# Two trunk layers on one core: attention given scheduler priority, S5's C products in alternation, softmax sums applied to the results

## The chip, the core and the metric

The kernel runs on one core of one Trainium2 chip (trn2). The time is device microseconds of one launch, from the first to the last instruction and the little that lies around them. Engines are TensorE (PE for its products, PEld for its weight loads), VectorE (DVE), ScalarE (ACT), GpSimd (POOL) and SyncE (SP), which here issues all transfers. TensorE's granted clock has two levels in the rows below, 1.2 and 2.4 GHz; the column PEclk shows them as 0.50 and 1.00, or a mixture over a stretch.

## What is computed

Two layers over 640 tokens of width 1024 (128 of a prompt, 512 of a sample grid of 8 rows by 64 columns). In each layer a normalised and modulated input goes through one projection (w_in); its parts feed three groups of heads; their outputs go through one projection (w_out), a normalisation, a SwiGLU feed-forward block and another normalisation. Cut to what matters here:

```python
def attend_dense(q, k, v):                      # GQA: 8 query heads, 2 key heads, 640 keys
    s = jnp.einsum('bqgrd,bkgd->bgrqk', qi, k) * scale
    p = jax.nn.softmax(s, axis=-1)
    return jnp.einsum('bgrqk,bkgd->bqgrd', p, v)
...
    # na_latent (NA): 4 heads, 256 local keys with a bias table and 128 context keys
    p = jax.nn.softmax(jnp.concatenate([s_loc, s_ctx], axis=-1), axis=-1)
    o = einsum(p_loc, vg) + einsum(p_ctx, cv)
...
    # ssm_mixer (S5): 16 groups of 16 channels, 64 complex states, two directions
    hs = ssm_scan(uf, lam_bar, b_bar, h0, rev)
    y = y + jnp.einsum('blgp,gcp->blgc', hs, c_mat).real
...
    o = jnp.concatenate([ssm_out, na_out, gqa_out], axis=-1) @ lp['w_out']
```

## The kernel before, in words

Tokens lie in 5 tiles of 128. Weights are split into two float32r halves, `wh` and `wl`, and three products (`mm3`, L311 to L313) make one. `Build.layer` runs a layer up to w_out, `Build.ffn` the rest; the second layer's modulation and S5 tables are made beside the first one's feed-forward block.

**The order of the work** is set by a scheduler at build time: each instruction has a priority by its place in the program, and among those that are ready in its own timeline the scheduler takes the one with the best priority. Each engine then runs its list in that order and waits at the head of it. So the program's order is a preference, and the lists that the build gives are the real order.

**The attention stage** of a layer is the part that the change touches. `layer` walks 18 GQA units through `pipelined` (L983 on), depth 1: the front of unit n, then the back of unit n-1, then `between`, which feeds in pieces of S5, of the remaining w_in products (`fill`), of the modulation (`ada`) and of the first layer's S5 tables. After that come 10 NA units, depth 2, with the rest of S5 between them, and then `wout`.

A GQA unit (`gqa_units.front`, L1139 on) takes a tile and two heads. For each head PE makes 128x640 scores (L1149) into one of two two-bank PSUM tiles `psS`; DVE takes the row maximum (L1152) and scales it (L1153); ACT makes the exponential with the row sum beside it (L1156); DVE takes the reciprocal (L1158), and POOL, or for one head of the second layer DVE, multiplies the 128x640 probabilities by it (L1162, L1160). The tables `SCG` and `SCN` choose that engine. The back (L1166 on) transposes the probabilities in ten 128x128 blocks through two PSUM tiles `psT` (helper L852), ACT copies them out (L1175), ten products with V follow (L1180; two heads in alternation on the two column halves of PE, 64 columns each), and ACT copies the 128x128 result (L1185). 32 of the 36 units are of this kind; four are a prompt's, of another form.

An NA unit (`na_units.front`, L926 on) is alike with 384 keys: scores L935, L936 and L940, exponentials L948, reciprocal L949, multiplication on POOL (L954) or DVE (L952), transposes, six products with V (L976, alternating too), and a split of the result from PSUM into a high half (ACT, L283) and a low half (DVE, L284). 16 units in the two layers are of this kind.

S5 (`ssm`, L669 on) walks 8 pairs of groups per layer. For a pair, PE makes the inputs (L714) and turns them (L724), DVE rotates, scans and rotates back (L732, L738, L742, L747, L748, L753), and `back` makes the C products (L767) and one product with the direct table (L769): for each of the two groups of the pair four products from a 64-row half of the state tile, then the direct one with 128 rows. The two groups write to two different banks of one `psS`:

```python
for gg in range(2):
    o, ps_ = yp[:, gg], slice(64 * gg, 64 * gg + 64)
    for n, (d, w) in enumerate(((0, 0), (0, 1), (1, 0), (1, 1))):
        nc.tensor.matmul(o, lhsT=sx[ps_, d, w, :], ...)
    nc.tensor.matmul(o, lhsT=ug[:, gg, :], ...)
```

A float32 product stands in the trace as two records; the counts below are of records.

Of the kernel before, what the change touches and what calls it, by code (L numbers as in the profile page):

```python
# [12 lines left out]
ALU = mybir.AluOpType  # L13
# [144 lines left out]
class Build:  # L158
# [510 lines left out]
    def ssm(self, l, zu, T, out):  # L669
# [90 lines left out]
        def back(pair, sx, rot, rml, tcb, tm, ug, vs, c):  # L760

            yp = self.psS()[0:NJ, :, 0:128]
            for gg in range(2):
                o, ps_ = yp[:, gg], slice(64 * gg, 64 * gg + 64)
                for n, (d, w) in enumerate(((0, 0), (0, 1), (1, 0), (1, 1))):
                    q = w * 2 + d
                    nc.tensor.matmul(o, lhsT=sx[ps_, d, w, :], rhs=tcb[ps_, q * 128:(q + 1) * 128], start=(n == 0),  # L767
                                     stop=False)
                nc.tensor.matmul(o, lhsT=ug[:, gg, :], rhs=tm[:, gg * 128:(gg + 1) * 128], start=False, stop=True)  # L769
# [63 lines left out]
    def softmax_prompt(self, sp, nh, P, scq):  # L833
# [13 lines left out]
        V.tensor_tensor(out=P, in0=P, in1=sm[:, 0:nh].unsqueeze(2).broadcast_to([128, nh, 128]), op=ALU.mult)  # L847

# [50 lines left out]
    def na_units(self, l, N, mh, ml):  # L899
# [26 lines left out]
        def front(cb):  # L926
# [23 lines left out]
            for hh in range(2):  # L950
                if self.SCN[l][hh]:
                    V.tensor_scalar(out=P[:, hh], in0=P[:, hh], scalar1=sm[:, hh:hh + 1], scalar2=None, op0=ALU.mult)  # L952
                else:
                    G.tensor_tensor(out=P[:, hh], in0=P[:, hh], in1=sm[:, hh:hh + 1].broadcast_to([128, 384]),  # L954
                                    op=ALU.mult)
            return P

        def back(cb, P):
# [8 lines left out]
            for j in range(3):  # L967
                for hh in range(2):
# [14 lines left out]
    def pipelined(self, units, depth, between=None):  # L983

        live = {}
        for n in range(len(units) + depth):
            if n < len(units):
                live[n] = units[n][0](units[n][2])
            if n >= depth:
                _, back, a = units[n - depth]  # L990
                back(a, live.pop(n - depth))
                if between:
                    between(n - depth)
# [97 lines left out]
    def gqa_units(self, l, kv, zq, K, ss, mixd):  # L1091
# [47 lines left out]
        def front(a):  # L1139
            i, pr = a  # L1140
            qT = prepare(i)
            Ps = []
            for hh in range(2):
# [7 lines left out]
                nm = self.small(1, tag="gm", bufs=4)  # L1151
                V.tensor_reduce(out=nm, in_=sp[:, :, 0:320], axis=AX.XY, op=ALU.max, negate=True)  # L1152
# [742 lines left out]
```

## Time and profile before

| | us |
|---|---|
| median of 3 runs | 1859.57 |
| lowest and highest | 1850.95, 1860.01 |
| the profiled execution, its own time | 1860.72 |
| its span, first to last instruction | 1858.9 |
| mean granted clock over the span | 0.927 of 2.4 GHz |

The span falls into these stretches, by the first and last instructions of each kind: the first layer's modulation and first w_in pieces up to about 125 us; its GQA units from 125 to 340; its NA units and the end of S5 from 340 to about 401, where products of w_out set in; w_out, feed-forward and the next layer's first pieces up to 1090; the second layer's GQA from 1090 to 1240, its NA and S5 from 1240 to 1312; w_out and feed-forward to the end. In the rows below a group of instructions shows its total busy time and the mean of one; "idle before" is the time that its engine stood idle just ahead of it, with what ended that.

### The profile page before, as it was taken

The numbers are of one execution on the slowest core, as the hardware profiler recorded it, in microseconds if no ns is written. First come the engines' busy times: TensorE is split into PE (matmuls) and PEld (weight loads), VectorE is DVE, ScalarE is ACT, GpSimd is POOL, SyncE is SP. The second block draws the span as 40 slices with busy tenths as digits, with TensorE's granted clock in tenths as the row PEclk, the third lists the DMA queues.
The fourth block names the chain that finished last, engine by engine and source line by source line (L and its number), as shares of the span: only waits on it lengthen the run. The fifth ranks groups of instructions, "written<-read, shape, count | busy, mean of one in ns | idle before, by whom it ended". The sixth has DMA issues, their size and how long they took to land. (4 is left out here: it accounts for less than half of the span.)

```text
span 1858.9 us, 31182 instructions
## 1 busy us (share of the span) xinstructions
PE 1694.2 (91%) x11432; PEld 1474.2 (79%) x11432; DVE 1257.5 (68%) x2468; ACT 820.5 (44%) x1780; POOL 847.6 (46%) x723
## 2 busy tenths in 40 slices
PE   5889798899699999999997989999989999999997
PEld 3878577678498879798886978877768898998996
DVE  5466634744758876687978577665467776777777
ACT  5335444554633334242336556544565242433433
POOL 4755524237642616054456344211594473553553
PEclk9879998769799999999999999985889999999999
DMA  8534765535534554432414343453452222312312
GB/s 302 132 93 113 218 197 156 150 121 168 183 107 142 167 158 151 130 110 91 126 57 156 110 110 99 108 159 80 156 189 84 91 83 77 103 58 79 103 57 80
DMA packets 183113, 234.87 MB, mean 126 GB/s; under 512 B 78960, under 2 KB 112048, under 8 KB 182960
## 3 DMA queue, kind: packets, MB, share of 16 engines
q1 hardware_dynamic: 182960, 232.88, 41.0%
q8 instruction: 90, 1.47, 0.3%
q14 instruction: 63, 0.52, 0.1%
HBM read 203.57 MB, written 29.39 MB: 125 GB/s over the span
## 5 line engine op out<-in xcount | busy, mean ns | idle before, releaser
L284 POOL TENSOR_TENSOR wl<-wr,wh 128x512 fp32r<-128x512 f32 x362 | 507.8, 1423 | 464.9 <-ACT wh L283 313.4
L283 ACT CAST wh<-wr 128x512 fp32r<-128x512 f32 x450 | 275.3, 619 | 394.4 <-PE psM L313 101.7
L311 PE MATMUL psM<-hh,wh 128*128 128x320 f32 x560 | 180.1, 322 | 8.9 <-DVE modc L393 2.6
L312 PE MATMUL psM<-hl,wh 128*128 128x320 f32 x560 | 178.3, 318 | 0.0
L313 PE MATMUL psM<-hh,wl 128*128 128x320 f32 x560 | 178.1, 318 | 0.0
L311 PEld LDWEIGHTS psM<-hh,wh 128*128 128x128 f32 x560 | 109.1, 195 | 12.5 <-DVE modc L393 2.8
L1162 POOL TENSOR_TENSOR ys<-ys,sm 128x640 f32<-128x640 f32 x48 | 61.7, 1289 | 120.4 <-DVE sm L1158 89.4
L311 PE MATMUL psT<-hh,wh 128*128 128x320 f32 x352 | 109.8, 312 | 0.0
L313 PEld LDWEIGHTS psM<-hh,wl 128*128 128x128 f32 x560 | 108.7, 194 | 1.4 <-issue 1.4
L312 PEld LDWEIGHTS psM<-hl,wh 128*128 128x128 f32 x560 | 109.0, 195 | 1.0 <-issue 0.7
L313 PE MATMUL psT<-hh,wl 128*128 128x320 f32 x352 | 109.0, 310 | 0.0
L312 PE MATMUL psT<-hl,wh 128*128 128x320 f32 x352 | 108.9, 309 | 0.0
L230 POOL TENSOR_TENSOR sm<-sm,mhalf 128x1 f32<-128x1 f32 (+2 forms) x46 | 54.7, 1191 | 94.2 <-DVE sm L260 53.6
L1152 DVE TENSOR_REDUCE sm<-psS 128x1 f32<-128x640 f32 x64 | 52.0, 819 | 56.0 <-PE psS L1149 55.6
L1629 DVE TENSOR_TENSOR ys<-ys,psM 128x320 f32<-128x320 f32 x140 | 64.9, 481 | 34.8 <-PE psM L313 32.9
L1629 DVE TENSOR_TENSOR ys<-ys,psT 128x320 f32<-128x320 f32 x140 | 65.0, 481 | 30.4 <-PE psT L313 29.3
L311 PE MATMUL psT<-b,wh 128*128 128x320 f32 x240 | 76.9, 320 | 8.9 <-DVE ys L1629 8.9
L852 PE MATMUL psT<-ident,ys 128*128 128x128 f32 x440 | 79.3, 304 | 6.1 <-ACT sm L1185 2.0
L284 POOL TENSOR_TENSOR wl<-ws,wh 128x512 fp32r<-128x512 f32 x40 | 53.7, 1344 | 63.7 <-ACT wh L283 63.7
L311 PE MATMUL psM<-b,wh 128*128 128x320 f32 x240 | 76.6, 319 | 6.2 <-DVE ys L1629 6.2
L311 PE MATMUL psT<-wh,xs 128*128 128x512 f32 x190 | 75.8, 399 | 2.9 <-DVE k L1753 2.9
L311 PE MATMUL psM<-wh,xs 128*128 128x512 f32 x190 | 75.0, 395 | 2.5 <-DVE k L1753 2.5
(438 smaller groups left out, 5071.8 us busy)
## 6 DMA issues: line engine op xcount, KB each, us to landing
wr<-in_w_ffn_in_dram SPq DMA_DIRECT2D x88, 512.0 KB, 3.7
ev<-in_w_ada_dram SPq DMA_DIRECT2D x112, 256.0 KB, 3.8
wr<-in_w_ffn_out_dram SPq DMA_DIRECT2D x40, 512.0 KB, 3.9
wr<-in_w_out_dram SPq DMA_DIRECT2D x32, 512.0 KB, 3.7
wr<-in_w_in_dram SPq DMA_DIRECT2D x28, 512.0 KB, 4.4
wa<-in_w_ada_dram SPq DMA_DIRECT2D x24, 512.0 KB, 5.7
k<-in_x_dram SPq DMA_DIRECT2D x10, 512.0 KB, 5.9
xs<-zqk SPq DMA_DIRECT2D x32, 160.0 KB, 3.8
```

The source lines that it names most:

```text
L230: self.nc.gpsimd.tensor_tensor(out=o, in0=v, in1=self.mhalf.broadcast_to([128, v.shape[1]]), op=ALU.pow)
L283: nc.scalar.copy(hi, src)
L284: (lo_eng or nc.vector).tensor_tensor(out=lo, in0=src, in1=hi.bitcast(F32), op=ALU.subtract)
L311: nc.tensor.matmul(ps, lhsT=ah, rhs=bh, start=first, stop=False)
L312: nc.tensor.matmul(ps, lhsT=ah, rhs=bl, start=False, stop=False)
L313: nc.tensor.matmul(ps, lhsT=al, rhs=bh, start=False, stop=last)
L852: self.nc.tensor.transpose(pt[:, j * 128:(j + 1) * 128], s, self.ident)
L1152: V.tensor_reduce(out=nm, in_=sp[:, :, 0:320], axis=AX.XY, op=ALU.max, negate=True)
L1162: G.tensor_tensor(out=P, in0=P, in1=sm.broadcast_to([128, 640]), op=ALU.mult)
L1629: V.tensor_tensor(out=o, in0=x, in1=y, op=ALU.add)
```

## The change

Three parts. First, the fronts and backs of the attention units and the preparation of queries (`preps`) are issued under a scheduler priority of 300, ahead of S5, the w_in pieces, the modulation and the tables. Second, S5's C products alternate between the two groups of a pair, and both direct products follow. Third, the probabilities are no longer divided by their row sums: a new helper, `over_sums`, spreads the reciprocals by two products with the identity into columns 384 to 511 of the PSUM tile that holds the unit's result, and the result is multiplied by them (GQA: ACT copies the result out, DVE multiplies it by the PSUM columns; NA: ACT copies the spread reciprocals out, DVE multiplies the result in PSUM, and the split follows as before). The multiplications L1162, L1160, L954 and L952 go; the two heads of a GQA unit share one reciprocal; the row maximum is written to a spare PSUM column.

```diff
@@ back (S5)
-            for gg in range(2):
-                o, ps_ = yp[:, gg], slice(64 * gg, 64 * gg + 64)
-                for n, (d, w) in enumerate(((0, 0), (0, 1), (1, 0), (1, 1))):
-                    q = w * 2 + d
-                    nc.tensor.matmul(o, lhsT=sx[ps_, d, w, :], rhs=tcb[ps_, q * 128:(q + 1) * 128], start=(n == 0),
-                                     stop=False)
-                nc.tensor.matmul(o, lhsT=ug[:, gg, :], rhs=tm[:, gg * 128:(gg + 1) * 128], start=False, stop=True)
+            for n, (d, w) in enumerate(((0, 0), (0, 1), (1, 0), (1, 1))):
+                q = w * 2 + d
+                for gg in range(2):
+                    ps_ = slice(64 * gg, 64 * gg + 64)
+                    nc.tensor.matmul(yp[:, gg], lhsT=sx[ps_, d, w, :], rhs=tcb[ps_, q * 128:(q + 1) * 128],
+                                     start=(n == 0), stop=False)
+            for gg in range(2):
+                nc.tensor.matmul(yp[:, gg], lhsT=ug[:, gg, :], rhs=tm[:, gg * 128:(gg + 1) * 128], start=False, stop=True)
@@ new helper
+    def over_sums(self, pt, r):
+
+        for h in range(2):
+            self.nc.tensor.matmul(pt[64 * h:64 * h + 64, 384:512], lhsT=r[:, h:h + 1].broadcast_to([128, 64]),
+                                  rhs=self.ident, start=True, stop=True, tile_position=(0, 64 * h))
@@ na_units
-            for hh in range(2):
-                if self.SCN[l][hh]:
-                    V.tensor_scalar(out=P[:, hh], in0=P[:, hh], scalar1=sm[:, hh:hh + 1], scalar2=None, op0=ALU.mult)
-                else:
-                    G.tensor_tensor(out=P[:, hh], in0=P[:, hh], in1=sm[:, hh:hh + 1].broadcast_to([128, 384]),
-                                    op=ALU.mult)
-            return P
+            return P, sm
...
+            self.over_sums(pt, sm)
+            rb = self.zt(128)
+            S.copy(rb, pt[:, 384:512])
+            V.tensor_tensor(out=pt[:, 256:384], in0=pt[:, 256:384], in1=rb, op=ALU.mult)
             a = slice(128 + cb * 128, 256 + cb * 128)
             self.split(pt[:, 256:384], mh[:, a], ml[:, a])
@@ pipelined (and the same around preps and the NA loop of layer)
+            with self.tc.high_priority(self.PRIO):
+                if n < len(units):
+                    live[n] = units[n][0](units[n][2])
+                if n >= depth:
+                    _, back, a = units[n - depth]
+                    back(a, live.pop(n - depth))
@@ gqa_units
-                nm = self.small(1, tag="gm", bufs=4)
-                V.tensor_reduce(out=nm, in_=sp[:, :, 0:320], axis=AX.XY, op=ALU.max, negate=True)
-                V.tensor_tensor(out=nm, in0=nm, in1=sch, op=ALU.mult)
+                nm, m = self.small(1, tag="gm", bufs=4), sp[:, 0, 320:321]
+                V.tensor_reduce(out=m, in_=sp[:, :, 0:320], axis=AX.XY, op=ALU.max, negate=True)
+                V.tensor_tensor(out=nm, in0=m, in1=sch, op=ALU.mult)
...
-                V.reciprocal(sm, sm)
-                if self.SCG[l][hh]:
-                    V.tensor_scalar(out=P, in0=P, scalar1=sm, scalar2=None, op0=ALU.mult)
-                else:
-                    G.tensor_tensor(out=P, in0=P, in1=sm.broadcast_to([128, 640]), op=ALU.mult)
+            V.reciprocal(sm, sm)
+            return Ps, sm
...
-            S.copy(outs[i][:, pr * 128:(pr + 1) * 128], pt[:, 256:384])
+            self.over_sums(pt, sm)
+            o = outs[i][:, pr * 128:(pr + 1) * 128]
+            S.copy(o, pt[:, 256:384])
+            V.tensor_tensor(out=o, in0=o, in1=pt[:, 384:512], op=ALU.mult)
@@ class constants
+    PRIO = 300
-    SCG = ((0, 0), (1, 0))
-    SCN = ((0, 0), (0, 1))
```

Where it moves instructions, the lists of the two builds show it. PE, the first layer, an S5 pair; of before (`k_473` is the pair's state tile, `k_474` its C table, L767 the C products, L769 the direct ones):

```order
998 L767 MATMUL psS_3059<-k_473_2541,k_474_2542 80x128 x4
999 L769 MATMUL psS_3059<-k_472_2540,k_440_2376 80x128
1000 L767 MATMUL psS_3059<-k_473_2541,k_474_2542 80x128 x4
1001 L769 MATMUL psS_3059<-k_472_2540,k_440_2376 80x128
1002 L1149 MATMUL psS_3145<-b_207_1134,xs_2991 128x320
```

and the same kind of place in the change's build, a later pair of that layer, among NA's scores (L942, L943, L947):

```order
1295 L943 MATMUL psS_3874<-mask 128x256
1296 L947 MATMUL psS_3874<-xs_3759,b_665_3726 128x192 x2
1297 L714 MATMUL psM_3852<-k_697_3842,k_433_2377 80x256 x2
1298 L767 MATMUL psS_3917<-k_658_3668,k_659_3669 80x128 x8
1299 L770 MATMUL psS_3917<-k_657_3667,k_433_2377 80x128 x2
1300 L859 MATMUL psT_3894<-ident,ys_3787 128x128
```

The eight C products of a pair stand in one run, and both direct ones behind them. Of the 16 pairs nine have the eight whole or one ahead of a run of seven; the others are cut into longer and shorter runs by attention and w_in.

POOL, the first layer's GQA units; of before (L1162 is the multiplication of the probabilities, L1080 the query's rotary sum, L703 and L705 S5's decay table):

```order
128 L1080 TENSOR_TENSOR xs_2990<-xs_2990,b_549_2992 128x256
129 L1162 TENSOR_TENSOR ys_2828<-ys_2828,sm_2829 128x640
130 L1162 TENSOR_TENSOR ys_2841<-ys_2841,sm_2842 128x640
131 L1162 TENSOR_TENSOR ys_3012<-ys_3012,sm_3013 128x640
132 L1162 TENSOR_TENSOR ys_3025<-ys_3025,sm_3026 128x640
133 L703 COPY k_586_3205<-r_65_310 128x320
```

and of the change, the same stretch:

```order
108 L1088 TENSOR_TENSOR xs_2976<-xs_2976,b_538_2978 128x256
109 L1088 TENSOR_TENSOR xs_3269<-xs_3269,b_591_3271 128x256
110 L703 COPY k_573_3189<-r_65_310 128x320
111 L705 MEMSET k_573_3189 128x2x2 x2
112 L284 TENSOR_TENSOR wl_3224<-wr_3221,wh_3223 128x512
```

The multiplications are gone from POOL's list, and nothing takes their place.

DVE, the first layer's first NA backs beside a pair of S5; of before (L742, L747, L748 and L753 are S5's scan and rotation, L284 the low half of NA's result, L288 a copy of transposed probabilities):

```order
435 L742 SCALAR_TENSOR_TENSOR k_714_3863<-k_712_3861,xs_2397 128x320
436 L747 TENSOR_TENSOR xs_2396<-k_714_3863,k_712_3861 128x320
437 L748 TENSOR_TENSOR xs_2396<-k_714_3863,k_712_3861 128x320
438 L945 TENSOR_REDUCE sm_3998<-ys_3984 128x2
439 L284 TENSOR_TENSOR hl_3788<-psT_3922,hh_3787 128x128
440 L753 TENSOR_TENSOR k_714_3863<-xs_2396 128x80 x4
```

and of the change (L983 is the new multiplication by the spread reciprocals):

```order
437 L742 SCALAR_TENSOR_TENSOR k_698_3843<-k_696_3841,xs_2389 128x320
438 L956 RECIPROCAL sm_3889<-sm_3889 128x2
439 L983 TENSOR_TENSOR psT_3900<-psT_3900,zt_3912 128x128
440 L747 TENSOR_TENSOR xs_2388<-k_698_3843,k_696_3841 128x320
441 L748 TENSOR_TENSOR xs_2388<-k_698_3843,k_696_3841 128x320
442 L288 COPY ys_3987<-psT_3994 128x256
443 L284 TENSOR_TENSOR hl_3772<-psT_3900,hh_3771 128x128
```

The result of an NA unit now has two steps on DVE, and the first of them stands ahead of the same pair's rotation back.

## Rows read from the trace of the kernel before

**Rows 1.** The page, engines: busy us, share of the span, instructions.

```profile
PE 1694.2 (91%) x11432; PEld 1474.2 (79%) x11432; DVE 1257.5 (68%) x2468; ACT 820.5 (44%) x1780; POOL 847.6 (46%) x723
```

**Rows 2.** Windows of attention: busy PE, PEld, DVE, ACT, POOL; PEclk, DMA share, GB/s.

```profile
125.00:340.00 215.00, 183.13 (x1620) 154.36 (x1620) 110.36 (x246) 96.75 (x241) 88.61 (x88) 0.90 0.56 162
340.00:401.00 61.00, 56.04 (x277) 41.19 (x275) 34.66 (x90) 29.41 (x83) 12.73 (x19) 0.64 0.36 100
1090.00:1240.00 150.00, 140.39 (x1152) 125.01 (x1152) 103.30 (x235) 90.93 (x230) 53.67 (x59) 0.95 0.40 107
1240.00:1312.00 72.00, 68.99 (x293) 52.29 (x292) 38.90 (x99) 31.95 (x89) 10.69 (x16) 0.53 0.42 111
```

**Rows 3.** The same view, the stretches at the lower clock at both stages' ends.

```profile
370.00:401.00 31.00, 30.91 (x138) 22.95 (x137) 13.21 (x39) 13.48 (x37) 6.31 (x6) 0.51 0.25 78
...
1242.00:1271.00 29.00, 28.53 (x104) 21.13 (x104) 15.13 (x35) 13.21 (x36) 2.91 (x9) 0.50 0.63 166
...
1274.50:1312.00 37.50, 36.39 (x159) 28.11 (x160) 18.40 (x54) 16.80 (x46) 5.67 (x5) 0.50 0.27 75
```

**Rows 4.** Who PE waited for, 125 to 340, then 1090 to 1240: us, times, longest.

```profile
PE psS L767 <- DVE k L753: 6.3, 2, 5.5
PE psS L1149 <- ACT ys L1156: 6.2, 3, 2.3
...
PE psS L1149 <- ACT ys L1156: 4.6, 2, 4.3
PE psS L767 <- DVE k L753: 2.5, 3, 1.3
```

**Rows 5.** S5's C products: the group, and the line with min/median/max ns.

```profile
L767 PE MATMUL psS<-k,k 64*80 64x128 f32 x256 | 54.6, 360 | 9.5 <-DVE k L753 8.8 <-ACT ys L1156 0.6
...
L767 PE MATMUL psS<-k,k x256: 269/417/500, 224.2 to 1294.4; 64*80 64x128 f32 x128
```

**Rows 6.** Timeline of PE at the full clock: start, us, what, records.

```profile
265.65 1.31 PE L1180 MATMUL psT<-b,b 128*64 128x128 f32 x20
...
357.62 1.10 PE L767 MATMUL psS<-k,k 64*80 64x128 f32 x8
358.64 0.45 PE L769 MATMUL psS<-k,k 128*80 128x128 f32 x2
...
365.04 0.88 PE L976 MATMUL psT<-ys,k 128*64 128x128 f32 x12
```

**Rows 7.** Timeline of PE at the half clock, the second layer's end of attention.

```profile
1257.09 1.99 PE L767 MATMUL psS<-k,k 64*80 64x128 f32 x8
1259.02 0.71 PE L769 MATMUL psS<-k,k 128*80 128x128 f32 x2
...
1276.27 1.12 PE L976 MATMUL psT<-ys,xs 128*64 128x128 f32 x8
1277.18 0.64 PE L976 MATMUL psT<-ys,k 128*64 128x128 f32 x4
1277.75 1.99 PE L767 MATMUL psS<-k,k 64*80 64x128 f32 x8
```

**Rows 8.** The multiplications of the probabilities on POOL, over the whole span.

```profile
L1162 POOL TENSOR_TENSOR ys<-ys,sm 128x640 f32<-128x640 f32 x48 | 61.7, 1289 | 120.4 <-DVE sm L1158 89.4
...
L954 POOL TENSOR_TENSOR ys<-ys,sm 128x384 f32<-128x384 f32 x24 | 21.7, 921 | 70.0 <-DVE sm L949 67.9 <-PE psM L824 2.1
```

**Rows 9.** Nearest rows for the added steps: 128x128 from PSUM on DVE and ACT.

```profile
L284 DVE TENSOR_TENSOR hl<-psT,hh 128x128 fp32r<-128x128 f32 x20 | 5.5, 283 | 14.2 <-ACT hh L283 14.2
L1185 ACT COPY sm<-psT 128x128 f32<-128x128 f32 x32 | 8.4, 262 | 8.7 <-PE psT L1180 6.0 <-DMA tabV<-ev 1.6 <-ACT xs L1087 0.8
```

**Rows 10.** Who PE waited for, 340 to 401.

```profile
PE psT L852 <- DVE hl L284: 2.1, 1, 2.1
```

**Rows 11.** One step of S5's rotation on DVE: the group, and the line.

```profile
L748 DVE TENSOR_TENSOR xs<-k,k 128x320 f32<-128x320 f32 x16 | 14.1, 882 | 0.0
...
L748 DVE TENSOR_TENSOR xs<-k,k x16: 476/485/1552, 218.3 to 1281.4; 128x320 f32<-128x320 f32 x16
```

More of the change, by code (lines that the diff above doesn't have):

```diff
@@ L949, in front, with back @@
             V.reciprocal(sm, sm)
-            for hh in range(2):
-                if self.SCN[l][hh]:
-                    V.tensor_scalar(out=P[:, hh], in0=P[:, hh], scalar1=sm[:, hh:hh + 1], scalar2=None, op0=ALU.mult)
-                else:
-                    G.tensor_tensor(out=P[:, hh], in0=P[:, hh], in1=sm[:, hh:hh + 1].broadcast_to([128, 384]),
-                                    op=ALU.mult)
-            return P
-        def back(cb, P):
+            return P, sm
+        def back(cb, front):
+            P, sm = front
             PT = self.big("ys").rearrange("p (j h q) -> p j h q", j=3, h=2)
@@ L986, in pipelined @@
         for n in range(len(units) + depth):
-            if n < len(units):
-                live[n] = units[n][0](units[n][2])
+            with self.tc.high_priority(self.PRIO):
[4 more added lines that the diff above has]
+                    back(a, live.pop(n - depth))
             if n >= depth:
-                _, back, a = units[n - depth]
-                back(a, live.pop(n - depth))
                 if between:
@@ L1141, in front @@
             qT = prepare(i)
-            Ps = []
+            Ps, sm = [], self.small(2, tag="gs", bufs=4)
             for hh in range(2):
@@ L1150, in front, with back @@
                                          rhs=kx[kv][:, b * 320:(b + 1) * 320], start=st, stop=en)
-                nm = self.small(1, tag="gm", bufs=4)
-                V.tensor_reduce(out=nm, in_=sp[:, :, 0:320], axis=AX.XY, op=ALU.max, negate=True)
-                V.tensor_tensor(out=nm, in0=nm, in1=sch, op=ALU.mult)
+                nm, m = self.small(1, tag="gm", bufs=4), sp[:, 0, 320:321]
+                V.tensor_reduce(out=m, in_=sp[:, :, 0:320], axis=AX.XY, op=ALU.max, negate=True)
+                V.tensor_tensor(out=nm, in0=m, in1=sch, op=ALU.mult)
                 P = self.ys(n=640)
-                sm = self.small(1, tag="gs", bufs=4)
                 S.activation(P.rearrange("p (b k) -> p b k", b=2), sp[:, :, 0:320], AF.Exp, bias=nm, scale=sch,
-                             accum_out=sm)
-                V.reciprocal(sm, sm)
-                if self.SCG[l][hh]:
-                    V.tensor_scalar(out=P, in0=P, scalar1=sm, scalar2=None, op0=ALU.mult)
-                else:
-                    G.tensor_tensor(out=P, in0=P, in1=sm.broadcast_to([128, 640]), op=ALU.mult)
+                             accum_out=sm[:, hh:hh + 1])
                 Ps.append(P)
-            return Ps
-        def back(a, Ps):
+            V.reciprocal(sm, sm)
+            return Ps, sm
+        def back(a, front):
             i, pr = a
+            Ps, sm = front
             PT5 = self.b5()
@@ L1408, in between @@
             if n + self.AHEAD < len(units):
-                preps[n + self.AHEAD][0](preps[n + self.AHEAD][1])
+                with self.tc.high_priority(self.PRIO):
+                    preps[n + self.AHEAD][0](preps[n + self.AHEAD][1])
         self.pipelined(units, 1, between)
@@ L1427, in layer @@
             if n < 10:
-                live[n] = units[n][0](units[n][2])
+                with self.tc.high_priority(self.PRIO):
+                    live[n] = units[n][0](units[n][2])
             for k in range(4):
@@ L1432, in layer @@
             if n >= depth:
-                units[n - depth][1](units[n - depth][2], live.pop(n - depth))
+                with self.tc.high_priority(self.PRIO):
+                    units[n - depth][1](units[n - depth][2], live.pop(n - depth))
                 for _ in range(self.SSMC[n - depth]):
```

## The prediction

> **What bounds the kernel now.** I read the page's engine rows first: PE is busy for 91% of the span, no other engine for more than 68% [rows 1]. A share over the whole span hides the stages, so I took windows of the two attention stages, the only place where the change does anything [rows 2]. The feed-forward blocks between them keep their lists but for small shifts, and what is saved ahead of them passes through to the end. In the four windows, 498 us in all, PE is busy for 448.6 and idle for 49.4: 31.9 in the first layer's GQA units, 9.6 in the second's, and only 5.0 and 3.0 in the two ends, where NA and the rest of S5 run. The reader should see three things there. POOL is nowhere near its limit. PE is the limit or close to it in three windows of four. And the ends run at the lower clock: three stretches of 31, 29 and 37.5 us show a PEclk of 0.50 or 0.51 with PE busy for 95.8 of 97.5 us [rows 3]. A product taken from those stretches is worth twice what it is worth at the full clock.
>
> Then I asked who PE waits for in its idle time [rows 4]. No row names POOL's multiplication of the probabilities: the scheduler has put other work between. Two kinds bear on the change: the exponentials that free the score buffers (6.2 and 4.6 us), and S5's rotation on DVE, on which the C products wait (6.3 and 2.5 us). Together 19.6 us. The rest are transfers, modulation vectors and single copies.
>
> **C products in alternation.** 256 records take 54.6 us of PE [rows 5]. Their durations run from 269 ns to a median of 417, mean 360: (360 - 269) / (417 - 269) = 0.61 of them ran at the half clock, ten pairs of 16. Eight records take 1.02 us from their start to the next kind at the full clock (357.62 to 358.64), 0.128 each [rows 6], and 1.93 at the half clock (1257.09 to 1259.02), 0.241 each [rows 7]. What they will take when they alternate between the two row halves of the array no row shows: before, the four products of one half always follow each other. The nearest rows are products that alternate between the two column halves: 12 records in 0.88 us, 0.073 each [rows 6], and 12 in 1.48 us at the half clock (1276.27 to 1277.75), 0.123 each [rows 7]. That is half or a little over, so two such products run side by side. With 16 records in a pair a full-clock pair saves 16 x 0.055 = 0.9 us, a half-clock pair 16 x 0.118 = 1.9: 6 x 0.9 + 10 x 1.9 = **24 us**. Bounds: nothing, if row halves do not run side by side, and 27.3, half of the 54.6. I take 24, by the column halves, whose products have the same type and length.
>
> The Trainium skill (TensorEngine Tiling (Array Packing), Key Properties) states that different tiles of the array can load weights and multiply in parallel, and the same page (Gotcha 1) that different row tiles cannot access one PSUM bank at the same time. Here the two groups write to two banks, so by the page the term is 24; had both results lain in one bank it would be about nothing, as in the second rival below. No row of this trace shows row halves in alternation.
>
> **Spread reciprocals.** 48 units get two float32 products more, four records each, 64 columns wide and alternating, like the products with V. By L1180, 20 records in 1.31 us, four cost 0.26 us at the full clock [rows 6]; 32 GQA units, nearly all at the full clock, 8.4 us. NA's 16 units I count half at either clock: 8 x 4 x 0.073 + 8 x 4 x 0.123 = 6.3 us. Sum **+15 us** of PE, between 12 (all at the full clock) and 20 (a third more for broken runs). It goes in full on the path, as everything on PE does here.
>
> **POOL's and DVE's multiplications go.** POOL loses 48 x 1.29 + 24 x 0.92 = 83 us [rows 8], half of its 165.7 us in the four windows [rows 2]; DVE loses 24 of its own kind and half the GQA reciprocals. As work they cost nothing now, since PE never waits for them by name, and I cost their removal at nothing. What does change is latency: the transposes no longer stand 1.3 us behind the exponential, and with the priority the scores, maxima and exponentials move ahead of S5, w_in and modulation in every list. That acts on the 10.8 us of waits for exponentials. S5's rotation gains too where POOL worked at the same time: L748, one of its steps, takes 485 ns in the median but 882 in the mean, with a longest of 1552 [rows 11], 6.4 us over 16 of them. The Trainium skill (GPSIMD Engine Reference, Specifications) states that POOL shares its SBUF interface with VectorE and that they contend when a VectorE instruction has two inputs in SBUF; L748 has two, so by that page these 6.4 us shrink with POOL's work, and the row agrees that something stretches it. Of the 19.6 us of such waits I take half, **-10 us**; the ends are 0 and 19.6.
>
> **Steps added to the backs.** A GQA unit gets one 128x128 step on DVE, an NA unit one on ACT and one on DVE; the nearest rows say 0.28 us on DVE and 0.26 on ACT [rows 9], 48 x 0.28 = 13 us and 16 x 0.26 = 4 us. DVE gives up 24 multiplications of 384 or 640 columns and 32 reciprocals, so its load hardly changes; neither engine is over 69% busy in a window of rows 2. I cost them at nothing behind PE's own work. If that cover is gone they cost what the first rival says. The output transfers of GQA wait 0.3 us longer; the SP list behind them has nothing that PE waits for at once. Writing the row maximum to PSUM I also cost at nothing: one number per row.
>
> **Sum.** -24 + 15 - 10 = -19 us against the profiled execution's 1860.7, so 1841.7; that execution lies 1.15 us above the median of the runs, and against the median I say **1841 us**. With the ends of the terms the forecast itself spans 1825 to 1853.
>
> **Rivals.**
>
> *The results' buffer is held longer (slower).* The unit's result sits in one of two `psT` tiles that the next unit's transposes need. Now it must wait for the two products, one step on ACT or DVE, and in NA for two steps on DVE that stand in line with S5's scan and rotation; in the list of the changed build L983 even stands ahead of the rotation back of the same pair, so that while it waits S5 waits, and the C products after it. For it: PE already waits once for 2.1 us for a low half on DVE, just before the long half-clock stretch at 370 us [rows 10]. Against it: the scheduler knows these steps, and in the first layer that was the one such wait in 61 us. Price: GQA 32 x (0.26 + 0.28) = 17 us, NA 16 x (0.39 + 0.26 + 0.28) = 15 us, and 16 x 0.9 = 14 us on S5, 46 in all. It ends above no change when over 19 of the 46 are seen, and slower by over 0.5% from 28. With three quarters of it, 34 us, the time is 1875.
>
> *The row halves do not run side by side.* Then the first term is nothing: +15 - 10 = +5, 1865 us. For it: no row shows it. Against it: the column halves do.
>
> *The clock.* Rows 3 show 95.8 us of PE's work at the half clock. PE had been short of work before those stretches (a gap at 367 to 369 us, see the wait of rows 10), and it did not recover while busy with small products. If denser C products and shorter waits let half of that work run at the full clock, 24 us more go: 1817 us; with all of it 48, 1793. For it: the change makes exactly these stretches denser. Against it: transposes, masks and 64-column products remain, and a new gap can start a new stretch as easily.
>
> **How the numbers follow.** The forecast gets 0.59, the clock 0.18, the held buffer 0.12, the row halves 0.11. A measurement of this kernel can tell about 0.5% from no change, that is 9 us: 1850 to 1869. Of the forecast's 0.59 I put 0.07 above 1850. Faster: 0.52 + 0.18 = 0.70. Same: 0.07 + 0.11 = 0.18. Slower: 0.12. The range, 1805 to 1866, holds the forecast, the row halves and most of the clock's case, and leaves out the held buffer and the clock's far end, some 0.18.
>
> **What would show it.** In the changed kernel's profile: L767's 256 records at some 27 us instead of 54.6, with eight in about 0.6 us at the full clock; the helper's products at 12 to 20 us; POOL lower by about 83 us; L748's mean nearer 0.5 us; PE idle for some 40 us in windows of the same stages. The first term is wrong if L767 still takes over 0.1 us a record at the full clock. The forecast as a whole is wrong if new waits of transposes for the added DVE steps exceed 20 us, or if the half-clock stretches at the ends of the stages change by more than a third in either direction.

## The result, and the profile after

The changed kernel takes 1805.6 us in the median of four runs (1797.3 to 1806.8), the kernel before beside it 1859.6: a ratio of 0.970 (95% interval 0.965 to 0.975), 54 us or 3.0% faster. The forecast was 1841 and the range 1805 to 1866. The sign and the parts of the mechanism that the forecast named are there; the size is not: 35 us more came than the sum has, and they came from the term that the sum left out, the granted clock. That the median lies inside the range, by 0.6 us, is luck: the forecast's own span ended at 1825. In all that follows a median is that of every run of a kernel, and a ratio leaves out three runs in a slower state (one of e2, one of e14 and one of the kernel before beside e13 and e14).

First the page's row of engines, which answers to [rows 1], in a profiled execution whose span is 1802.7 us (1858.9 before):

```profile
PE 1655.2 (92%) x11624; PEld 1447.3 (80%) x11624; DVE 1224.2 (68%) x2460; ACT 822.3 (46%) x1796; POOL 762.5 (42%) x651
```

PE has 192 records more and 39 us less of busy time; POOL has 85 us less, of which the multiplications were 83. Next the windows of the changed kernel, in the columns of [rows 2]: the same four stages, cut at round numbers, and then the four longest stretches at the lower clock in the two ends, which answer to [rows 3].

```profile
125.00:310.00 185.00, 168.02 (x1669) 144.55 (x1670) 101.68 (x238) 96.45 (x242) 47.38 (x56) 0.95 0.61 175
310.00:372.00 62.00, 53.65 (x337) 40.50 (x336) 39.57 (x110) 32.65 (x94) 5.43 (x10) 0.78 0.57 155
1050.00:1200.00 150.00, 142.84 (x1253) 127.62 (x1252) 85.59 (x225) 91.80 (x235) 32.02 (x42) 0.97 0.41 111
1200.00:1252.00 52.00, 45.23 (x287) 34.10 (x286) 33.73 (x94) 30.95 (x90) 5.67 (x10) 0.80 0.54 148
...
323.00:333.00 10.00, 9.20 (x41) 6.60 (x42) 7.05 (x13) 6.20 (x17) 0.91 (x5) 0.50 0.83 167
353.50:370.50 17.00, 17.00 (x73) 13.17 (x72) 7.06 (x16) 11.04 (x27) 3.03 (x2) 0.50 0.29 92
1207.00:1213.50 6.50, 6.50 (x32) 4.68 (x31) 3.45 (x6) 2.85 (x10) 0.59 (x3) 0.50 0.91 232
1224.00:1237.50 13.50, 13.08 (x73) 10.59 (x74) 9.40 (x37) 4.59 (x18) 0.00 (x0) 0.50 0.37 109
```

The four stages take 449 us instead of 498: 49 of the 56 us by which the spans differ. PE is idle for 39.3 us in them, against 49.4. The granted clock in the two ends is 0.78 and 0.80 where it was 0.64 and 0.53, and where the three stretches of [rows 3] alone were 97.5 us long, these four are 47.

Then the groups that the terms named: L767 is the C products, L853 the spread reciprocals, L748 and L742 steps of S5's rotation on DVE, L1192 the new division of GQA's result.

```profile
L767 PE MATMUL psS<-k,k 64*80 64x128 f32 x256 | 27.0, 311 | 0.2 <-DVE k L753 0.2
L853 PE MATMUL psT<-ident,sm 128*64 128x128 f32 x192 | 20.0, 284 | 0.0
...
L742 DVE TENSOR_TENSOR_SCAN k<-k,xs 128x320 f32<-128x320 f32 x16 | 13.1, 821 | 0.9
L1192 DVE TENSOR_TENSOR sm<-sm,psT 128x128 f32<-128x128 f32 x32 | 9.1, 284 | 14.4 <-ACT sm L1191 14.1
L748 DVE TENSOR_TENSOR xs<-k,k 128x320 f32<-128x320 f32 x16 | 8.8, 551 | 0.0
```

To say how much of a stage is work, clock and waiting, I took the granted clock in windows of 1 us from the first score of a layer's GQA units to its first product with w_glu (125.2 to 406.5 and 1086.0 to 1314.6 us before; 125.8 to 372.2 and 1052.4 to 1256.8 after). A window's busy time by 2 x (1 - PEclk) is its busy time at the half clock; half of that is what the clock costs, and busy time less that half is the work as it would be at the full clock. Idle, clock cost and work add up to the length.

| four stages, us | length | idle | busy at the half clock | its cost | work at the full clock |
|---|---|---|---|---|---|
| before | 509.9 | 51.6 | 159.8 | 79.9 | 378.4 |
| changed | 450.8 | 37.7 | 71.9 | 35.9 | 377.4 |

Work did not shrink: the denser C products pay for the spread reciprocals and no more. Waiting gave 14 us, the clock 44.

A profile is one execution. The record has the span and the mean granted clock of every execution, and the span times what its clock lacks of 1.00 is what the lower clock takes in the whole of it, idle time at that clock included. For the kernel before that is 130 to 136 us in the mean on the four chips (single executions 118 to 149), for the changed kernel 88 (86 to 90). So the clock's share holds over the executions, while 10 us between two single profiles can be the spread of one kernel.

### The profile page after: what moved, and what is told of

The parts are those of the page before. It is cut to its first block, busy times and chain, and to the rows that moved or that the text cites. A ratio compares the mean times of both kernels' runs of the same rounds, so it can differ in the third digit from the quotient of the medians.

```text
span 1802.7 us, 31473 instructions
## 1 busy us (share of the span) xinstructions
PE 1655.2 (92%) x11624; PEld 1447.3 (80%) x11624; DVE 1224.2 (68%) x2460; ACT 822.3 (46%) x1796; POOL 762.5 (42%) x651
## 4 chain that ended last, share of the span: by engine, by line
PE 66%; DVE 12%; DMA 10%; ACT 4%; issue 3%; POOL 2%; SPq 1%; POOLq 0%; DVEq 0%; ACTq 0%
PE psM L311 9%; PE psM L312 9%; PE psM L313 9%; PE psT L311 6%; PE psT L312 6%; PE psT L313 5%; DMA ev<-in_w_ada_dram 3%; PE psT L859 3%; PE psS L311 2%; PE psS L312 2%; PE psS L313 2%; PE psS L1157 2%; DMA wr<-in_w_ffn_in_dram 2%; PE psT L1184 2%; POOL wl L284 2%
## 5 line engine op out<-in xcount | busy, mean ns | idle before, releaser
L284 POOL TENSOR_TENSOR wl<-wr,wh 128x512 fp32r<-128x512 f32 x362 | 502.1, 1406 | 523.8 <-ACT wh L283 341.6
L1160 DVE TENSOR_REDUCE psS<-psS 128x1 f32<-128x640 f32 x64 | 52.8, 828 | 45.3 <-PE psS L1157 43.7
L284 POOL TENSOR_TENSOR wl<-ws,wh 128x512 fp32r<-128x512 f32 x40 | 53.6, 1341 | 62.7 <-ACT wh L283 62.6
L311 PE MATMUL psM<-wh,hh 128*128 128x256 f32 (+1 forms) x232 | 73.8, 318 | 6.1 <-DVE sm L1329 2.9
L859 PE MATMUL psT<-ident,ys 128*128 128x128 f32 x440 | 75.4, 291 | 2.7 <-ACT ys L290 1.0
```

What stands on the lines that cost most here:

```text
L284: (lo_eng or nc.vector).tensor_tensor(out=lo, in0=src, in1=hi.bitcast(F32), op=ALU.subtract)
L311: nc.tensor.matmul(ps, lhsT=ah, rhs=bh, start=first, stop=False)
L859: self.nc.tensor.transpose(pt[:, j * 128:(j + 1) * 128], s, self.ident)
L1160: V.tensor_reduce(out=m, in_=sp[:, :, 0:320], axis=AX.XY, op=ALU.max, negate=True)
```

## The experiments

Each part alone and each part taken out, then kernels that ask why the clock rose. The table has the medians, the ratio to the kernel before on the same chip (its medians there: 1862.2 for e1 to e4, 1858.9 for e5 to e8, 1864.3 for e9 to e12, 1857.5 for e13 and e14), and the four stages of the profiled execution as above.

| kernel | us | ratio, 95% interval | stages | idle | half clock | work |
|---|---|---|---|---|---|---|
| e1 alternation alone | 1812.3 | 0.974 (0.970 to 0.978) | 457.6 | 59.4 | 61.3 | 367.6 |
| e2 row sums alone | 1839.7 | 0.989 (0.985 to 0.993) | 489.7 | 41.7 | 122.3 | 386.8 |
| e3 priority alone | 1837.6 | 0.988 (0.984 to 0.992) | 484.1 | 41.7 | 122.2 | 381.3 |
| e4 changed, no priority | 1812.0 | 0.973 (0.969 to 0.977) | 457.2 | 45.4 | 83.0 | 370.4 |
| e5 alternation, products twice | 1848.1 | 0.994 (0.992 to 0.996) | 502.6 | 65.0 | 104.8 | 385.3 |
| e6 old order, half the products | 1837.8 | 0.989 (0.984 to 0.994) | 485.2 | 52.4 | 141.7 | 362.0 |
| e7 alternation and priority | 1806.9 | 0.974 (0.969 to 0.979) | 454.4 | 43.6 | 79.8 | 370.9 |
| e8 changed, no alternation | 1829.7 | 0.985 (0.979 to 0.990) | 462.1 | 36.5 | 60.9 | 395.1 |
| e9 changed, POOL's work back | 1811.8 | 0.971 (0.967 to 0.975) | 450.9 | 39.2 | 69.4 | 377.1 |
| e10 changed, row sums in GQA only | 1799.1 | 0.966 (0.961 to 0.971) | 444.9 | 34.3 | 69.6 | 375.9 |
| e11 e10, priority in GQA only | 1796.6 | 0.963 (0.959 to 0.968) | 443.9 | 34.0 | 68.6 | 375.6 |
| e12 changed, again | 1806.6 | 0.969 (0.965 to 0.972) | 448.9 | 35.8 | 69.4 | 378.4 |
| e13 before, 128-row products added | 1845.1 | 0.994 (0.990 to 0.997) | 491.4 | 41.8 | 105.0 | 397.2 |
| e14 alternation in pairs 4 to 7 | 1825.0 | 0.980 (0.975 to 0.985) | 470.4 | 54.9 | 90.4 | 370.3 |

### The three parts, alone and left out: e1 to e4, e7, e8

e1 is the kernel before with the hunk of the diff at L760 and nothing else; e2 with the row sums (no SCG and SCN, `over_sums` and the divisions in the backs); e3 with the five `high_priority` lines. e4, e7 and e8 are the changed kernel without one of them each.

> The kernel before with the C products in alternation and nothing else. By the forecast's own terms: 24 us less than before (1836), L767 at some 27 us, idle time of PE as before. By the clock theory (denser products lift the ends of the attention stages out of the half clock by themselves): some 14 us of work and at least 30 us of clock, 1815 or less, with the two ends (340 to 401 and 1240 to 1312 us of before) at a granted clock near 0.8 instead of 0.64 and 0.53. By the gap theory (the half clock starts in a gap of PE, and the gaps come from the chain score, maximum, exponential, multiplication, transpose): the gaps stay, so the half clock stays, and it gives 24 us or less, 1836 to 1845.

> The kernel before with the row sums divided out of the result (no multiplication of the probabilities, spread reciprocals instead) and nothing else. By the forecast's terms: 15 us more of PE's work and 5 to 10 us of waits less, so 1865 (between 1855 and 1875). By the gap theory: the multiplication's 1.3 us leave every chain and POOL's work no longer stretches DVE's steps, the gaps in the first layer's GQA units shrink, and the half clock with them: some 25 us less in that stage against 15 us of work, so 1845 to 1855. L748 falls from 882 ns to about 550 if POOL's work stretched it.

> The kernel before with the scheduler's priority for the fronts and backs of attention and nothing else. By the forecast: no work changes, waits change by 10 us at most, 1850 to 1860. By the gap theory with the order as its cause: the gaps of PE in 215 to 225 and 285 to 292 us are filled, the half clock behind them goes, some 25 to 30 us less, 1830 to 1835. If S5 and w_in are starved by it, slower: over 1865.

> The changed kernel without the priority: alternation and row sums alone. If the parts add up by the forecast's terms: 24 less, 15 more, some waits less: 1846 to 1850. If priority is what closed the gaps of the first layer's GQA units: that stage stays near 215 us instead of 183, and the time is 1835 or more. If alternation and shorter chains did it together: within 10 us of the changed kernel's 1806.

> Alternation and priority, with the multiplications of the probabilities as in the kernel before (no spread reciprocals). If the gains were independent: 1862 - 50 - 24 = 1788. If each takes its gain from the same stock of half-clock time, of which the alternation leaves 61 us: 1800 to 1808, and with 15 us less work on PE than the changed kernel it may be the faster one; if the shorter chains of the row sums are needed as well, 1808 to 1815.

> The changed kernel without the alternation. Independent gains: 1862 - 22 - 24 = 1816. One stock of half-clock time, with no products that fill both halves: row sums and priority overlap too, 1825 to 1835. The forecast's own terms (15 us of work against 10 of waits): 1865.

The alternation alone gives 50 us, nearly as much as the whole change. These are its windows: the four stages, then the last end's two stretches at the lower clock.

```profile
123.10:321.10 198.00, 167.70 (x1607) 141.97 (x1607) 106.98 (x238) 96.52 (x240) 88.17 (x88) 0.94 0.59 171
321.10:378.50 57.40, 48.13 (x323) 35.81 (x320) 39.72 (x105) 32.38 (x95) 14.73 (x22) 0.82 0.50 139
1062.20:1205.60 143.40, 132.14 (x1134) 118.26 (x1136) 97.42 (x229) 89.59 (x225) 50.81 (x57) 0.96 0.42 111
1205.60:1264.40 58.80, 50.33 (x337) 37.69 (x333) 43.19 (x108) 32.94 (x97) 14.22 (x19) 0.85 0.57 151
...
1216.00:1229.50 13.50, 13.50 (x54) 9.65 (x55) 7.66 (x14) 6.52 (x17) 2.17 (x6) 0.50 0.78 192
1240.00:1243.50 3.50, 3.48 (x28) 2.78 (x30) 3.50 (x14) 2.41 (x11) 0.83 (x1) 0.52 0.28 75
```

It takes 10.8 us of work and 49.3 us of clock cost away ((159.8 - 61.3) / 2), and gives 7.8 us back as idle time; together these are the 52.3 us by which its stages are shorter. For the alternation the gap theory, by which the half clock would stay because its gaps stay, falls: there is more idle time and far less half clock.

Row sums and priority alone give 22 and 25 us, e2 although it adds 8.4 us of work: both take 10 us of waiting and 19 us of clock cost. That is where the forecast and I were wrong about e2, and where the priority was worth more than "waits by 10 us at most". For these two the gap theory came near: it said 1845 to 1855 for e2 and 1830 to 1835 for e3, and they took 1839.7 and 1837.6. Alone the three parts give 50 + 22 + 25 = 97 us, together 54. They draw on one stock, the 80 us that the clock costs. With the alternation in place, row sums add nothing that can be told (e4 against e1, ratios 0.973 and 0.974; changed against e7, 0.970 and 0.974), and priority 6 us or nothing (changed against e4, 0.970 and 0.973; e7 against e1, 0.974 both), all within the intervals. Without it (e8) the other two give 29.

e8 also says what the alternation is worth beside the other two: 24 us, from 1829.7 to 1805.6, half of what it is worth alone. In the profile of e8, with the C products in the old order, only 60.9 us are left at the half clock, as few as in e1, and its longest stretch there is as short as the changed kernel's:

```profile
330.50:347.50 17.00, 16.64 (x62) 12.36 (x62) 8.57 (x17) 7.75 (x22) 1.35 (x6) 0.50 0.59 132
```

That profile is one of the two fastest of e8's four executions. By the mean of the four the lower clock takes 100 us of the span (89 to 114), where it takes 132 in the kernel before, 87 in e1 and 88 in the changed kernel. So on top of the other two the alternation brought about 12 us of clock and 13 of everything else, a rough split with so wide a spread.

### Why the clock rose: e5, e6, e13, e14

The alternation does two things at once: it keeps both row halves of the array at work, and it is over sooner. e5 keeps the first and takes back the second (each product issued twice), e6 the reverse (old order, two of four products left out), e13 fills rows without shortening anything. For e13:

```
             for gg in range(2):
                 o, ps_ = yp[:, gg], slice(64 * gg, 64 * gg + 64)
+                for _ in range(2):
+                    nc.tensor.matmul(o, lhsT=ug[:, gg, :], rhs=tm[:, gg * 128:(gg + 1) * 128], start=True, stop=True)
                 for n, (d, w) in enumerate(((0, 0), (0, 1), (1, 0), (1, 1))):
```

In e5 the loop of the changed kernel runs over the four (d, w) twice, with start at 0 and 4; in e6 the old loop runs over ((0, 0), (1, 1)) alone.

> The kernel before with the C products in alternation and each of the eight issued twice (the first round is overwritten by the second), so that the alternation costs PE about what the products of the kernel before cost at the full clock: 512 records by some 0.064 us, 33 us, where 256 records by 0.13 took 33. If the alternation alone gained 49 us because it takes less time: that is given back, 1850 or more. If it gained because products that fill both row halves let the granted clock rise sooner: only their own 16 to 18 us come back, 1826 to 1832, and busy time at the half clock in the four attention stages stays near 61 us instead of 160.

> The kernel before with its C products in the old order, but only two of the four of each group (the other two are left out of the output), so PE has as little to do there as with the alternation, and the array is still filled by one row half at a time. If it is the shorter time that counts: as the alternation alone, 1812 (1805 to 1820). If it is the filled array: the 17 us of work at the full clock go and little of the clock's share, 1835 to 1845, with over 110 us of PE's busy time in the four stages still at the half clock.

> The kernel before with the C products in the old order, and two products of all 128 rows (the one with Z, issued twice more and overwritten) ahead of each group's four: PE gets 128 records more, by L769's 18.7 us over 64 some 17 to 22 us of work at the full clock. If filled rows alone raise the granted clock: PE's busy time at the half clock in the four stages falls from 160 to below 125 us, which pays for the added work, and the time is 1850 to 1865. If it does not, because what counts is how soon the thin products are over: half-clock time stays or grows, and the time is 1878 to 1900.

> The kernel before with the alternation in the last four of the eight pairs of each layer only, which run mostly in the ends where NA runs. The alternation gained 12.2 us in the first GQA stage, 13.7 in the first end, 5.8 and 20.6 in the second layer's. If each stage gains by its own products: the ends' 34 us stay and the GQA stages' 18 go, 1825 to 1832, the first GQA stage back at 210 us. If the first GQA stage gained by chance of where its gaps fall: it stays near 198 and the time is 1812 to 1818.

In e13 PE has 18.8 us more work in the four stages, and the kernel is 12 us faster (interval 5 to 19). The group of its added products, and its last end in four windows:

```profile
L766 PE MATMUL psS<-k,k 128*80 128x128 f32 x128 | 22.5, 299 | 1.4 <-ACT ys L1158 1.4
```

```profile
1233.20:1246.50 13.30, 10.95 (x79) 8.33 (x76) 9.37 (x21) 4.63 (x16) 3.58 (x3) 1.00 0.79 236
1246.50:1267.00 20.50, 20.31 (x77) 14.79 (x77) 13.12 (x27) 10.81 (x28) 3.78 (x10) 0.50 0.58 125
1267.00:1291.00 24.00, 20.93 (x169) 16.01 (x165) 15.55 (x49) 12.61 (x36) 0.83 (x1) 1.00 0.35 100
1291.00:1301.00 10.00, 9.06 (x35) 7.14 (x36) 5.60 (x14) 6.10 (x20) 4.78 (x4) 0.50 0.23 66
```

Set these beside two windows of the kernel before that stand just ahead of its two long stretches there, which begin at about 1240.5 and at 1274.5 us [rows 3]:

```profile
1235.20:1240.50 5.30, 4.03 (x32) 3.14 (x28) 5.14 (x9) 2.01 (x8) 3.23 (x3) 0.99 0.43 124
...
1271.00:1274.50 3.50, 2.06 (x21) 1.49 (x20) 3.50 (x8) 1.50 (x4) 1.26 (x1) 0.99 0.00 0
```

In both PE is short of work for 1.3 to 1.4 us, and then the clock goes to 1.2 GHz. In the kernel before it stays there for 30.5 and 37.5 us though PE is busy for 97 to 98% of them; in e13, with 128-row products between the groups, it is back at 2.4 GHz after 20.5 and stays for 24.

The first layer's end says otherwise. There e13 has a stretch at the half clock of 40.9 us, longer than any of the kernel before in these stages, with 12 of the added records and 32 of the C products in it (the second and third row are those of L766 and of L769, here the C products: PE, PEld, PEclk, DMA):

```profile
328.40:369.30 40.90, 39.17 (x158) 30.35 (x159) 21.67 (x52) 16.45 (x46) 5.83 (x12) 0.50 0.49 120
328.40:369.30 40.90, 3.27 (x12) 2.56 (x12) 0.50 0.49 120
328.40:369.30 40.90, 7.97 (x32) 6.48 (x32) 0.50 0.49 120
```

Of the 55 us that e13 has less at the half clock, 43 are the second layer's (35.4 for 78.4) and 12 the first's (69.6 for 81.3). In e6 the second layer's end reads:

```profile
1222.50:1253.00 30.50, 29.43 (x112) 21.63 (x114) 19.82 (x46) 14.89 (x43) 4.21 (x11) 0.50 0.65 172
1260.00:1290.50 30.50, 30.41 (x127) 23.50 (x127) 14.81 (x43) 15.49 (x40) 5.80 (x5) 0.50 0.30 93
```

Half as many thin products, and the two stretches are still 30.5 us each. In e5, with 7 us more work than before but both halves in use, no stretch of either layer is longer than 20.5:

```profile
334.90:355.40 20.50, 17.31 (x80) 13.19 (x82) 11.16 (x24) 7.03 (x22) 2.97 (x8) 0.50 0.32 85
1280.40:1300.90 20.50, 19.32 (x80) 15.35 (x81) 10.69 (x22) 13.07 (x32) 5.37 (x5) 0.50 0.26 87
```

So without any saving of work e5 has 55 us less at the half clock than the kernel before, and e13 55 less with more work still. Shortness counts too: of the alternation's gain only 16 to 18 us were expected to come back in e5, and it was 36 (1812.3 to 1848.1), which lies nearer to the 1850 of the other reading. In the stages of the two profiles it is 45: 17.7 of work, 22 of clock cost (43.5 us more at the half clock) and 5.6 of idle time. Either alone gives 11 or 21 us, both together 50. More than that these runs do not show. e2, e3 and e8 leave the C products as they were and have 38, 38 and 99 us less at the half clock than the kernel before, e3 by the order of the lists alone. How much of e5's and e13's 55 us came by such shifts no run says. By the means over all executions the lower clock takes 132 us in the kernel before, 120 in e6, 112 in e2 and e3, 108 in e5 and 104 in e13. What raises the clock in a given stretch stays open.

e14 suggests that the gain lies mostly at the products' own place: the ends keep their gain (118.8 us together, against 150.5 before and 116.2 in e1), and the second GQA stage, whose products are in the old order, is back at 151.5 (149.2 and 143.4). The first GQA stage is not: 200.1, with 210.2 before and 198.0 in e1. That stage is shorter than before in every run, e6 (200.0) and e13 (201.4) too; some 10 us there came with any of these edits, so they can't be put down to one part of the change.

### POOL's work, and a faster version: e9 to e12

> The changed kernel in which POOL multiplies the probabilities after all, 48 times in GQA and 24 in NA, but behind the transposes, where nothing reads them any more: POOL's 83 us of work are back, the chain to the transposes stays short, and the results are divided as in the changed kernel. If the row sums help because POOL's work no longer stretches DVE's steps: L748 rises from 551 ns to 700 or more and L742 from 821 to 950, and the time by 8 to 20 us, to 1815 to 1825. If they help by the shorter chain alone, or not at all: 1803 to 1809.

> The changed kernel with the row sums divided out of GQA's results only; NA multiplies its probabilities as in the kernel before. By the stages of the runs so far (NA's ends take 65.0 and 63.4 us in the changed kernel, 58.7 and 60.8 with alternation and priority alone, GQA's first stage 183.0 against 196.3): 5 to 12 us less than the changed kernel, 1794 to 1801. If these differences of the ends are chance of where the gaps fall: 1803 to 1809.

> As the run before, and with the priority on GQA's units alone (the loop over NA and the rest of S5 in the old priority). Alternation without priority had the shortest ends, 57.4 and 58.8 us: 10 to 14 us less than the changed kernel, 1792 to 1796. If chance: 1803 to 1809. If NA needs the priority: 1810 or more.

> The changed kernel once more, as the standard for the three runs beside it: 1803 to 1809, with about 70 us of PE's busy time in the four stages at the half clock.

e9 puts POOL's multiplications behind the transposes, in place on the probabilities, which no one reads any more. It takes 1811.8, the changed kernel beside it 1806.6; the intervals overlap, so removing 83 us of POOL's work is worth 5 us or nothing here. Steps of S5 on DVE felt it, the scan and L747 most, and not the one that the forecast named. In e9:

```profile
L742 DVE TENSOR_TENSOR_SCAN k<-k,xs 128x320 f32<-128x320 f32 x16 | 16.4, 1026 | 0.6
L747 DVE TENSOR_TENSOR xs<-k,k 128x320 f32<-128x320 f32 x16 | 10.7, 667 | 0.2
```

In the changed kernel they took 821 and 488 ns; L748 stays at 554. In e2, where POOL's multiplications are gone and the rest of the change is missing, L748 was at 686, not at the 550 expected. Why L748 moved is seen in the timeline of the kernel before (start, us, engine): its records take either 0.48 or 1.55 us.

```profile
314.83 1.36 POOL L1162 TENSOR_TENSOR ys<-ys,sm 128x640 f32<-128x640 f32 x1 [1.54 <-DVE sm L1158]
314.99 1.54 DVE L748 TENSOR_TENSOR xs<-k,k 128x320 f32<-128x320 f32 x1
...
334.61 0.48 DVE L748 TENSOR_TENSOR xs<-k,k 128x320 f32<-128x320 f32 x1
```

Six of 16 were long, and POOL was busy for 1.2 us or more beside each of the six (three times with L1162, three times with a split of weights) and beside none of the ten short ones; in the changed kernel one of 16 is long, beside a split of weights. This agrees with the Trainium skill (GPSIMD Engine Reference, Specifications), which has POOL share its SBUF interfaces with VectorE and contend with VectorE instructions that have two SBUF inputs. Nor is it always DVE that is stretched: in e9 one L748 took 0.47 us while a sum on POOL beside it (L1092, from 218.67 us) took 1.50, where 0.74 is its median. What counts is whether the two meet, and which of them gives way, not how much POOL does.

e10 and e11 follow the stages: NA's ends took 63.4 and 65.0 us in the changed kernel but 60.8 and 58.7 in e7, which multiplies there. With the multiplications back in NA, and in e11 the old priority there, the times are 1799.1 and 1796.6, 7 and 10 us under the changed kernel on the same chip. They are the fastest kernels here, but their intervals (0.961 to 0.971, 0.959 to 0.968) touch the changed kernel's (0.965 to 0.972); that they beat it is likely and not settled. In their profiles the first end takes 64.6 and 62.9 us, the second 59.9 and 57.7: only the second end gained.

## Why the prediction was right or wrong

**C products in alternation, -24 us: the step that failed, by its size.** The price of the products themselves was right. In the changed kernel's timeline two runs of C products at the full clock read:

```profile
344.41 1.10 PE L767 MATMUL psS<-k,k 64*80 64x128 f32 x14
345.44 0.67 PE L770 MATMUL psS<-k,k 128*80 128x128 f32 x4
...
348.29 0.89 PE L767 MATMUL psS<-k,k 64*80 64x128 f32 x12
```

14 records in the 1.03 us up to the next kind and 12 in 0.89 are 0.074 each, as the column halves said (0.073), and the group takes 27.0 us: row halves do run side by side. The Trainium skill has it so too (TensorEngine Tiling (Array Packing), Key Properties). But the step counted only what those 256 records would save, with the clock of each stretch left as it was. Alone (e1) the edit shortened the stages by 52 us: 11 of work and 49 of the clock's cost, less 8 of new idle time. Beside the other two parts it gave 24 (e8), the number of the forecast, but by another sum: about 12 of clock and 13 of the rest. What the sum lacked is the clock, 44 us in the changed kernel, which the prediction had as a rival. Two figures of the prediction do not go with its own terms: 54.6 less 24 is 30.6, not the "some 27" for L767, and the upper end of its span, 1859.6 - 24 + 20, is 1856, not 1853. Neither changes the result.

**The clock, 24 to 48 us at a chance of 0.18.** This is what happened: 44 us in the four stages, near its far end in microseconds, and 55% of the 79.9 that the half clock cost there. The prediction's own sign of being wrong came with it: the stretches at the stages' ends, 119 us together before, were 51, a change of more than a third. Its other signs came as forecast. Two things in the step were wrong. It priced 95.8 us of half-clock work, the three longest stretches; the four stages held 159.8. And it gave the change's own mechanism a low chance because "a new gap can start a new stretch as easily". Gaps did start new stretches (ten in the stages before, nine after); the stretches became shorter, a longest of 17 us for one of 37.5. The rows for that were there: [rows 3] show PE busy for nearly the whole of stretches in which the clock did not return, so being busy was not enough, and what else could end such a stretch was the thing to ask. The runs show that it can be shortened in several ways, and leave open by what.

**Spread reciprocals, +15 us.** Their products take 20.0 us busy, the upper end. But the forecast had them on the path in full; in e2 the stages' work grew by 8.4, and e2 is 22 us faster. On top of alternation and priority the whole part is worth 1 us by the medians and 7 by the ratios, within the uncertainty.

**Multiplications gone, waits -10 us.** Idle time fell by 10.1 in the windows of [rows 2], 13.9 in the stages as cut above: about right. In the first GQA stage the wait of scores for an exponential fell from 6.2 to 2.3 us and that of the C products for the rotation from 6.3 to 0.2; in the second the first of these is 4.0 for 4.6 and the other, 2.5, is gone. PE's waits in the first:

```profile
PE psM L381 <- DMA wa<-in_w_ada_dram: 5.0, 4, 3.2
PE psM L386 <- ACT zt L385: 5.0, 2, 3.1
PE psS L1157 <- ACT ys L1163: 2.3, 1, 2.3
...
PE psT L859 <- DVE sm L1192: 0.9, 1, 0.9
...
PE psS L767 <- DVE k L753: 0.2, 1, 0.2
```

POOL's work itself at nothing: e9 bears it out within 5 us.

**Steps added to the backs, nothing, and the rival of the held buffer.** The only such waits among the longest that the view names in the four windows are 0.9 us for L1192, in the row above, and 0.5 for a low half in the last window; the rival needed 28. It falls, and so does the one of the row halves.

**Priority, only by way of waits.** Alone it gave 25 us, 10 of waiting, 19 of clock cost and 3 us of work moved into the stages. The forecast had no term for it.

Work -1, waiting -14 and clock -44 make up the 59.1 us between the two profiles' stages. They do so by the way they are taken, so they say where the time went, and not that a sum could have had the 44 beforehand.

## What to carry to other kernels

Where a stretch runs at the lower clock although the engine is busy, price an edit there by what it does to the stretch, not by the time of the instructions it touches: split each stage into idle time, clock cost and work before summing. Products that use half of the array's rows can alternate between the halves, here with results in two banks: that brought a record from 0.128 to 0.074 us at the full clock, and was worth 50 us alone, where the stages' work fell by 11, and 24 beside the other two parts. Parts that each feed on the same lost time do not add (97 us apart, 54 together), so price them as a set, and look whether a part is still needed once the strongest is in: for the row sums no gain could be told. And look at several executions before putting 10 us of clock down to an edit.

## What the hardware showed unexpectedly

Adding work made a kernel faster: 128 records of 128-row products, 22.5 us of PE, took 12 us off the kernel before (e13). PE can be busy for 36.39 of 37.50 us at 1.2 GHz without the clock coming back [rows 3], and in e13 for 39.17 of 40.90, with 128-row products among the C products. The longest such stretch of the attention stages was 20.5 us or less in e1, e5, e8 and the changed kernel, and 27 to 41 in e2, e3, e6, e7 and e13. e8 has the old order and e7 the alternation, so the order of the C products alone does not tell the two groups apart. And a step on DVE with two inputs in SBUF (L748) takes 0.48 us or 1.55, with nothing between in the kernels before and after; in these two it was long where POOL was at work beside it.
